# A hybrid encoder block on one core: the mixer's projections and chains in another order, and the small-weight terms of the half products last

## The chip, the cores and the metric

The kernel runs on one NeuronCore of a Trainium2 chip. The metric is the device time of one execution in microseconds (us); lower is better. The core's engines work through instruction lists of their own, each in its order, and wait for each other by semaphores: PE (TensorE, matmuls; its weight loads are counted apart as PEld), DVE (VectorE), ACT (ScalarE), POOL (GpSimd) and SP (SyncE, which issues the weights' DMAs).

## The reference

One encoder block on 512 tokens and 16 learned meta tokens (528 in all), model width 1024, all in float32:

```python
h = h + 0.5 * swiglu(rms_norm(h, ffn1_norm), w_gate1, w_up1, w_down1)      # D_FF = 2816
u = rms_norm(h, mix_norm)
z = u @ w_in                                   # split into 10 parts, below
y_a = hgrn2_bidir(zq_a, zi_a, zf_f, zf_b, zg_a, ...)   # 4 heads of 128, chunks of 128, both directions
y_b = axial_gqa(zq_b, zk_b, zv_b, q_norm, k_norm, cos, sin)   # 8 query heads of 64, 2 key heads
mixed = sigmoid(zgate_a) * (y_a @ w_up_a) + sigmoid(zgate_b) * (y_b @ w_up_b)
h = h + mixed @ w_out
h = h + 0.5 * swiglu(rms_norm(h, ffn2_norm), w_gate2, w_up2, w_down2)
return h[:, N_META:]
```

## The kernel before

Activations lie transposed, features on the 128 partitions and tokens along the free axis. Every weight and activation of a product is split into a large part (`whi`, `xh`: float32 rounded to float32r) and the small rest (`wlo`, `xl`); a product is three matmuls, hi x xh, hi x xl and lo x xh. A weight block of 128 x 1024 is loaded by SP, its `whi` is cast by ACT and its `wlo` subtracted by DVE (`Weights`); two buffers of each.

**The FFNs.** Hidden columns come in groups; all but the first four use a Strassen-like scheme with seven products of halves for gate (i = 0) and up (i = 1) each (`pair`, `step`, `product`). `product` is twelve matmuls into one PSUM bank: four blocks kk of 128 rows, three terms each. Outside the mixer a scheduler orders the instructions of each engine.

**The mixer** is ordered by a planner while the program is written (`Order`, called `il`). It keeps a clock `t` for PE and a time at which each other engine is free; `account` adds an estimated cost per instruction, `HOP` is its estimate for passing a result to another engine and `DRAIN` for a matmul's result to be there. The main stream is the projections `u @ w_in` (`group`, 24 matmuls for 512 tokens, or twice as many narrower ones for all 528, which need two of the three `mm` banks of PSUM). Chains are Python generators: `prepare` (norms and rotary positions of queries and keys, values), `scores` (matmul into bank S, softmax), `turned` (transposes of the probabilities into `at`, product with the values into an `mm` bank, `ta`, `yb`), `gla` (the recurrence: per head seven levels, each a matmul `gs<-Z,ks`, DVE updates of Z, tot and A, and ACT's copy `ks`), `gla_finish`. `tick` after each three terms of a projection lets every chain step that is ready by then be written (`pump`); `need` makes the main stream stand still until a condition holds. So the planner alone sets the order of every engine's list in the mixer; at run time the engines follow these lists.

The main stream before: the queries' projection of head 0, keys, backward gate, values, forward gate and the rest of head 0; then per head hd an output gate's projection (`early`), the wait for the scores of head hd - 2, and that head's six projections. At its end, the wait for `attention`, the split of all four `yb` into `ybh` and `ybl`, and eight products with them (`branch`), gated by `mixb`.

Of the kernel before, what the change touches and what calls it, by code (L numbers as in the profile page):

```python
# [32 lines left out]
WARM = 12  # L33
LEVELS = (1, 2, 4, 8, 16, 32, 64)
# [119 lines left out]
class Chain:  # L154


    def __init__(self, gen, ready):
        self.gen, self.ready, self.eng, self.wait = gen, ready, None, None


class Order:
# [4 lines left out]
    HOP, DRAIN = 0.12, 0.3  # L166
# [7 lines left out]
    def account(self, eng, op, args, kw):  # L174
# [15 lines left out]
        if eng == "act":  # L190
            d = n * 0.000916 + 0.115
            if "accum_out" in kw:
                d += 0.2
            if not isinstance(kw.get("scale", 1.0), (int, float)):
                d += 0.17
# [18 lines left out]
    def add(self, gen):  # L214
        self.chains.append(Chain(gen, self.cur.ready))
# [21 lines left out]
    def tick(self, _=None):  # L237
        self.pump()
# [54 lines left out]
def block_kernel(tc, xT, wg1, wu1, wd1, w_in, wup, wout, wg2, wu2, wd2, params,  # L293
# [5 lines left out]
    def group(outs, w, xs, tick=None):  # L299
        hi, lo = w  # L300
        n = len(xs)
        for k in range(n):
            sl = slice(k * P, (k + 1) * P)
            xh, xl = xs[k]
            for i, (a, b) in enumerate(((hi, xh), (hi, xl), (lo, xh))):
                for o, cols in outs:
                    pe.matmul(o, a[:, sl], b[:, cols], start=(k == 0 and i == 0),  # L307
                              stop=(k == n - 1 and i == 2))
            if tick:
                tick(0.65 if len(outs) == 1 else 0.68)  # L310

    with (tc.tile_pool(name="persist", bufs=1) as sp, tc.tile_pool(name="wts", bufs=1) as wp,
# [157 lines left out]
        def pair(ft, xq, n):  # L470
# [113 lines left out]
        with tc.tile_pool(name="f1", bufs=1) as ft:  # L584
# [40 lines left out]
            order = [Z_QB, Z_KB, Z_FB, Z_VB, Z_FF, Z_QA, Z_G, Z_I]  # L625
            for hd in range(1, HEADS):
                order += [Z_GB + hd - 2] if hd > 1 else []
                order += [c + hd for c in (Z_QB, Z_FB, Z_FF, Z_QA, Z_G, Z_I)]
            plan = [w_in[c] for c in order]
            tiles = [w_in[Z_GB + c] for c in range(KT)] + [wup[c][:, 512:] for c in range(KT)]  # L630
            plan += tiles[HEADS - 2:EARLY] + tiles[KT:KT + 5] + tiles[EARLY:KT] + tiles[KT + 5:]
# [7 lines left out]
        with tc.tile_pool(name="mix", bufs=1) as mp, tc.manual_schedule(engines={pe.engine}):  # L639
# [3 lines left out]
            def zcols(n):  # L643
# [6 lines left out]
                group(outs, w, um, il.tick)  # L650
# [11 lines left out]
            def weights():  # L662
# [4 lines left out]
                w = W.ready.pop(0)  # L667
                if not W.ready:
# [6 lines left out]
                return w  # L675
# [36 lines left out]
            with (tc.tile_pool(name="heads", bufs=1) as hp, tc.tile_pool(name="small", bufs=1) as mn,  # L712
# [3 lines left out]
                oml, noml = lower_bounds()  # L716
# [619 lines left out]
```

## Time and profile before

| | |
|---|---|
| median of 3 runs | 1191.2 us (1189.47 to 1192.89) |
| the profiled execution | 1190.44 us, span of the trace 1188.6 us |
| busy time of PE / DVE / ACT / POOL | 1166.7 / 865.0 / 578.5 / 98.6 us |
| mean granted TensorE clock | 0.997 |
| the mixer in the trace | from 376.6 to about 727 us |

Busy time is the union of an engine's records. Matmuls are pipelined and their ends are modelled, so a busy PE is not always PE at its steady pace; the time from one start to the next tells that.

### The profile page before, as it was taken

How to read it: one execution, taken by the hardware profiler on the slowest of the kernel's cores; microseconds unless marked ns; L12 is line 12 of the kernel's file. 1: busy time of each engine (PE TensorE's matmuls, PEld its weight loads, DVE VectorE, ACT ScalarE, POOL GpSimd, SP SyncE). 2: the span in 40 equal slices, each digit the busy share in tenths (PEclk: the TensorE clock that was granted, in tenths of full speed). 3: DMA queues.
4: the chain of work that ended last, by engine and by line, in shares of the span. 5: the costliest groups of instructions: out<-in, count | busy, mean ns of one | idle time of the engine just before them, and what ended most of it. 6: DMA issues, size and time to landing. Idle time of an engine off the chain costs nothing.

```text
span 1188.6 us, 19335 instructions
## 1 busy us (share of the span) xinstructions
PE 1166.7 (98%) x7765; PEld 1068.4 (90%) x7765; DVE 865.0 (73%) x1409; ACT 578.5 (49%) x981; POOL 98.6 (8%) x77
## 2 busy tenths in 40 slices
PE   8999999999999999999999989999999999999998
PEld 8999999999999889888888868888879998998997
DVE  7988848847956779797886855454888956966863
ACT  5545525524545366757657553334444634533541
POOL 1001001001103000000000000213001101101100
PEclk9999999999999999999999999999999999999999
DMA  6233322322223221112111012332423233323213
GB/s 235 63 97 133 98 90 89 113 83 107 68 67 116 75 86 57 51 37 71 37 54 53 28 45 98 107 109 95 142 64 132 85 106 110 105 91 109 90 56 123
DMA packets 34233, 106.21 MB, mean 89 GB/s; under 512 B 3936, under 2 KB 4320, under 8 KB 34144
## 3 DMA queue, kind: packets, MB, share of 16 engines
q1 hardware_dynamic: 33984, 104.44, 26.4%
q8 instruction: 61, 1.00, 0.3%
q0 software_dynamic: 160, 0.54, 0.1%
q14 instruction: 28, 0.23, 0.1%
HBM read 102.87 MB, written 2.10 MB: 88 GB/s over the span
## 4 chain that ended last, share of the span: by engine, by line
PE 90%; DVE 5%; ACT 2%; DMA 2%; issue 1%; SPq 0%; POOL 0%; ACTq 0%; DVEq 0%
PE mm L289 21%; PE mm L307 20%; PE mm L484 14%; PE at L484 9%; PE at L307 5%; PE am L307 4%; PE gs L484 4%; PE S L307 4%; PE gs L289 3%; PE am L484 2%; DVE wlo L102 1%; PE S L289 1%; PE at L289 1%; DMA raw<-in_wu 1%; ACT whi L101 1%
## 5 line engine op out<-in xcount | busy, mean ns | idle before, releaser
L101 ACT CAST whi<-raw 128x1024 fp32r<-128x1024 f32 (+2 forms) x179 | 149.9, 839 | 254.2 <-PE mm L307 87.3
L102 DVE TENSOR_TENSOR wlo<-raw,whi 128x1024 fp32r<-128x1024 f32 (+2 forms) x179 | 176.9, 991 | 22.1 <-ACT whi L101 20.0
L289 PE MATMUL mm<-xh,whi 128*128 128x512 f32 (+1 forms) x352 | 115.1, 364 | 1.6 <-DVE tm L289 1.2
L289 PE MATMUL mm<-xh,wlo 128*128 128x512 f32 (+1 forms) x352 | 108.8, 346 | 0.0
L289 PE MATMUL mm<-xl,whi 128*128 128x512 f32 (+1 forms) x352 | 108.6, 346 | 0.0
L102 DVE TENSOR_TENSOR wlo<-sums,whi 128x1024 fp32r<-128x1024 f32 x72 | 87.5, 1217 | 25.3 <-ACT whi L101 25.2
L101 ACT CAST whi<-sums 128x1024 fp32r<-128x1024 f32 x72 | 75.4, 1050 | 62.0 <-DVE sums L128 21.0
L133 POOL TENSOR_TENSOR sums<-raw 128x512 f32<-128x512 f32 x36 | 57.9, 1608 | 495.1 <-DVE wlo L102 485.8
L289 PEld LDWEIGHTS mm<-xh,whi 128*128 128x128 f32 x352 | 62.4, 191 | 9.9 <-DVE tm L289 2.0
L289 PEld LDWEIGHTS mm<-xh,wlo 128*128 128x128 f32 x352 | 62.0, 191 | 8.4
L289 PEld LDWEIGHTS mm<-xl,whi 128*128 128x128 f32 x352 | 62.1, 191 | 4.9
L307 PE MATMUL mm<-hh,wlo 128*128 128x256 f32 (+1 forms) x218 | 63.0, 334 | 0.0
L307 PE MATMUL mm<-hh,whi 128*128 128x256 f32 (+1 forms) x218 | 62.9, 333 | 0.1
L307 PE MATMUL mm<-hl,whi 128*128 128x256 f32 (+1 forms) x218 | 62.9, 332 | 0.0
L484 PE MATMUL mm<-xl,whi 128*128 128x264 f32 (+1 forms) x216 | 61.3, 284 | 0.0
L484 PE MATMUL mm<-xh,whi 128*128 128x264 f32 (+1 forms) x216 | 61.2, 284 | 0.0
L484 PE MATMUL mm<-xh,wlo 128*128 128x264 f32 (+1 forms) x216 | 61.2, 283 | 0.0
L289 ACT CAST whi<-raw 128x1024 fp32r<-128x1024 f32 (+1 forms) x41 | 39.6, 965 | 38.9 <-PE mm L289 32.5
L307 PE MATMUL mm<-xl,whi 128*128 128x512 f32 (+2 forms) x152 | 51.1, 362 | 1.3 <-DVE xl L389 1.3
L307 PE MATMUL mm<-xh,whi 128*128 128x512 f32 (+2 forms) x152 | 50.4, 357 | 1.8 <-ACT xh L388 1.8
L578 DVE SCALAR_TENSOR_TENSOR h<-mm,h 128x512 f32<-128x512 f32 (+2 forms) x40 | 20.9, 544 | 41.4 <-PE mm L307 41.3
L289 DVE TENSOR_TENSOR Z<-Z,tot 128x512 f32<-128x512 f32 (+1 forms) x48 | 40.7, 875 | 13.8 <-PE gs L289 6.8
(354 smaller groups left out, 3593.2 us busy)
## 6 DMA issues: line engine op xcount, KB each, us to landing
raw<-in_wg SPq DMA_DIRECT2D x43, 512.0 KB, 3.6
raw<-in_wu SPq DMA_DIRECT2D x43, 512.0 KB, 3.3
raw<-in_w_in SPq DMA_DIRECT2D x42, 512.0 KB, 3.2
raw<-in_wd SPq DMA_DIRECT2D x48, 384.0 KB, 3.1
raw<-in_wd SPq DMA_DIRECT2D x16, 256.0 KB, 2.6
raw<-in_wup SPq DMA_DIRECT2D x16, 256.0 KB, 2.6
raw<-in_wout SPq DMA_DIRECT2D x8, 512.0 KB, 3.3
h<-in_xT SPq DMA_DIRECT2D x4, 528.0 KB, 5.7
```

What stands on the lines that cost most here:

```text
L101: nc.scalar.copy(hi[:, c], src)
L102: nc.vector.tensor_tensor(lo[:, c], src, hi[:, c].bitcast(F32), ALU.subtract)
L133: nc.gpsimd.tensor_tensor(t[:, E], r0[:, E], r1[:, E], ALU.add)
L289: return f(*args, **kw)
L307: pe.matmul(o, a[:, sl], b[:, cols], start=(k == 0 and i == 0), stop=(k == n - 1 and i == 2))
L484: pe.matmul(o, a[:, sl], b[:, kk, :], start=(start and kk == 0 and i == 0), stop=(kk == 3 and i == 2), skip_group_check=True)
L578: dve.scalar_tensor_tensor(h[c][:, cols], o, 0.5, h[c][:, cols], ALU.mult, ALU.add)
```

## The change

Three things are altered. In `product` the four matmuls with the weight's small part come after the eight with its large part. In the planner, the costs are other ones (HOP and DRAIN, two of ACT's, DVE taken as busy until 6.5 us after the start), ready chains are looked for after every matmul instead of every third, and of chains that are ready, the two of the recurrence win by a lead of 5 us. And the mixer's program is another: the projections follow a list (`MAIN`: q, k, w are queries, keys, values, b, f, a, g, i the recurrence's, s an output gate), the wait for a head's scores moves from the main stream into the chain of the queries (`queries_rest`), the sum of a head's two halves becomes a chain of its own (`summed`), the split of a head's output follows at once (`parted`, into buffers that are free by then: `kh0` and `kl0`, `cossin`, two `qst`), and the first branch begins with three heads before the fourth is there.

```diff
-    HOP, DRAIN = 0.12, 0.3
+    HOP, DRAIN = 0.06, 0.12
...
     def pump(self):
         while self.chains:
-            ch = min(self.chains, key=self.ready)
+            ch = min(self.chains, key=lambda ch: self.ready(ch) - (ch.lead if self.ready(ch) <= self.t else 0.0))
...
             for i, (a, b) in enumerate(((hi, xh), (hi, xl), (lo, xh))):
                 for o, cols in outs:
                     pe.matmul(o, a[:, sl], b[:, cols], start=(k == 0 and i == 0),
-                              stop=(k == n - 1 and i == 2))
-            if tick:
-                tick(0.65 if len(outs) == 1 else 0.68)
+                              stop=(k == (HEADS if ks else n) - 1 and i == 2))
+                if tick:
+                    tick()
...
-                for kk in range(4):
-                    sl = slice(half * 512 + kk * P, half * 512 + (kk + 1) * P)
-                    for i, (a, b) in enumerate(((hi, xh), (hi, xl), (lo, xh))):
-                        pe.matmul(o, a[:, sl], b[:, kk, :], start=(start and kk == 0 and i == 0),
-                                  stop=(kk == 3 and i == 2), skip_group_check=True)
+                terms = [(kk, hi, x) for kk in range(4) for x in (xh, xl)] + [(kk, lo, xh) for kk in range(4)]
+                for i, (kk, a, b) in enumerate(terms):
+                    pe.matmul(o, a[:, half * 512 + kk * P:half * 512 + (kk + 1) * P], b[:, kk, :],
+                              start=(start and i == 0), stop=(i == 11), skip_group_check=True)
...
+MAIN = """q0 k0 b0 f0 a0 w0 g0 i0 b1 f1 q1 a1 g1 i1 q2 s0 q3 s1 b2 f2 a2 g2 i2 b3 f3 a3 g3 i3 s2""".split()
...
                     act.activation(tq[:, :SEQ], z[:, :SEQ], AF.Square)
+                    if j > 1:
+                        yield lambda: f"att{j - 2}" in il.done
...
-                            yield
-                            act.copy(t[d], av[s])
-                            yield
-                            dve.tensor_tensor(yb[j][d], av[d], t[d], ALU.add)
-                            give()
+                            il.add(summed(j, e, av, t, d, s))
...
+                def parted(j):
+
+                    yield lambda: {"att1", f"q{HEADS - 1}", f"att{j}"} <= il.done
...
+                    act.copy(both[0], yb[j])
+                    yield
+                    dve.tensor_tensor(both[1], yb[j], both[0].bitcast(F32), ALU.subtract)
...
-                for hd in range(1, HEADS):
-                    if hd > 1:
-                        early(hd - 2)
-                        il.need(lambda: f"att{hd - 2}" in il.done)
-                    queries(hd)
-                    for _ in gla_inputs(hd):
-                        pass
...
-                il.need(lambda: "attention" in il.done)
-                YB = []
-                ybh = hp.tile([P, 4, SEQ], F32R, name="ybh", tag="ph")
-                ybl = hp.tile([P, 4, SEQ], F32R, name="ybl", tag="pl")
...
+                il.need(lambda: f"y{HEADS - 2}" in il.done)
+                begun = [branch(range(HEADS - 1), go_on=c + 1 < BEGUN) for c in range(BEGUN)]
+                il.need(lambda: f"y{HEADS - 1}" in il.done)
```

Where this moves instructions is seen in the engines' lists. A row is the line of the kernel, the operation, out<-in and the shape, with the engines that it waits for.

First PE's list in an FFN, where a later group of hidden columns begins: before, the end of the gate's second product (`mm<-b21`) and the beginning of up's first (`at<-b11`):

```order
L484 MATMUL mm<-b21h,whi 128x264
L484 MATMUL mm<-b21l,whi 128x264
L484 MATMUL mm<-b21h,wlo 128x264
L484 MATMUL at<-b11h,whi 128x264 [waits Activation_49]
L484 MATMUL at<-b11l,whi 128x264
L484 MATMUL at<-b11h,wlo 128x264 [waits DVE_49]
```

After, the end of up's first product and the beginning of its second (`am<-b21`); three more pairs `at<-b11h,whi` and `at<-b11l,whi` stand ahead of these rows:

```order
L485 MATMUL at<-b11h,whi 128x264
L485 MATMUL at<-b11l,whi 128x264
L485 MATMUL at<-b11h,wlo 128x264 [waits DVE_49]
L485 MATMUL at<-b11h,wlo 128x264 x3
L485 MATMUL am<-b21h,whi 128x264
L485 MATMUL am<-b21l,whi 128x264
```

The wait for DVE, which makes `wlo`, stood at the third matmul of the product and stands at the ninth.

Then PE's list in the mixer behind the product of head 0's second half with its values (`pmeta` is the last matmul of that). Before:

```order
L289 MATMUL mm<-pmeta,vs_4869 128x512 [waits DVE_49]
L289 MATMUL gs<-Z,ks 128x128 [waits DVE_49,Activation_49]
L289 MATMUL gs<-Z,ks 128x128 x3
L289 MATMUL at<-ident,pr 128x128 x4
L289 MATMUL am<-ident,pr 16x128
L289 MATMUL S<-kh_4807,qst 128x256
L289 MATMUL S<-kh_4807,qst 128x272
L289 MATMUL S<-kl_4808,qst 128x256
L289 MATMUL S<-kl_4808,qst 128x272
L289 MATMUL mm<-ident,on 128x128 [waits DVE_49,Activation_49]
L289 MATMUL mm<-ident,on 128x128 [waits Activation_49] x3
L289 MATMUL mm<-kones,tq 128x2 [waits Activation_49]
```

After:

```order
L291 MATMUL mm<-pmeta,vs_4854 128x512
L291 MATMUL gs<-zi,ks 128x128 [waits DVE_49,Activation_49]
L291 MATMUL gs<-zi,ks 128x128 x3
L291 MATMUL mm<-xh,whi 128x512
L291 MATMUL mm<-xl,whi 128x512
L291 MATMUL mm<-xh,wlo 128x512
L291 MATMUL mm<-vt,A 128x128 [waits DVE_49]
L291 MATMUL mm<-vt,A 128x128
L291 MATMUL mm<-st,Z 128x128 x2
L291 MATMUL mm<-vt,A 128x128 x2
```

Before, a level of the recurrence, the next transposes, scores, `on` and the norm `kones` of the next queries follow with no projection (`mm<-xh,whi`) among them. Now projection matmuls stand behind the recurrence's first product; the outputs (`vt,A`), one score and a norm follow, 22 matmuls, and then projections again.

Last PE's list where the attention ends. Before, from the last matmul of the last head's output to the first branch:

```order
L289 MATMUL mm<-pmeta,vs_4870 128x512 [waits DVE_49]
L289 MATMUL mm<-vt,st 128x128
L289 MATMUL mm<-vt,on 128x128 [waits Activation_49]
L289 MATMUL mm<-vt,on 128x128 x3
L289 MATMUL mm<-ybh,whi 128x512 [waits PE_49,Activation_49]
L289 MATMUL mm<-ybl,whi 128x512 [waits DVE_49]
L289 MATMUL mm<-ybh,wlo 128x512
```

After, in the first branch, which begins behind the last head's output with one projection matmul, four transposes of Z and two projection matmuls between (`kh`, `kl` and `cossin` hold heads 0 and 1, `qst` heads 2 and 3):

```order
L291 MATMUL mm<-kh_6440,whi 128x512
L291 MATMUL mm<-kl_6441,whi 128x512
L291 MATMUL mm<-kh_6440,wlo 128x512
L291 MATMUL mm<-cossin,whi 128x512 x2
L291 MATMUL mm<-cossin,wlo 128x512
L291 MATMUL mm<-qst,whi 128x512 x2
L291 MATMUL mm<-qst,wlo 128x512
L291 MATMUL mm<-ident,Z 16x128 [waits DVE_49]
L291 MATMUL mm<-qst,whi 128x512 [waits Activation_49]
L291 MATMUL mm<-qst,whi 128x512 [waits DVE_49]
L291 MATMUL mm<-ident,Z 128x128 x4
L291 MATMUL mm<-qst,wlo 128x512
```

Before, each head's large and small part is waited for in turn, all four of them; after, only the last head's two parts are, behind nine matmuls with the other three. In ACT's list the four casts `ybh<-yb` stood together; now one cast `qst<-yb` stands there. The norm of the first queries (`kones`) stands behind twelve pairs of matmuls of the keys' projection before and behind ten after.

## Rows read from the trace of the kernel before

**Rows 1.** The page's busy time: engine, busy us (share of the span), instructions.
```profile
PE 1166.7 (98%) x7765; PEld 1068.4 (90%) x7765; DVE 865.0 (73%) x1409; ACT 578.5 (49%) x981; POOL 98.6 (8%) x77
```

**Rows 2.** Windows: stretch, length, PE, PEld, DVE, ACT, POOL busy (instructions), PEclk, DMA.
```profile
376.60:393.10 16.50, 15.04 (x87) 13.54 (x86) 12.27 (x30) 6.50 (x11) 2.09 (x6) 0.90 0.30 104
...
389.70:393.00 3.30, 3.30 (x17) 3.30 (x17) 1.83 (x10) 0.08 (x1) 0.00 (x0) 0.50 0.29 109
...
476.00:516.00 40.00, 37.14 (x233) 31.46 (x232) 30.23 (x62) 26.28 (x57) 0.22 (x2) 1.00 0.09 34
...
684.00:708.00 24.00, 19.92 (x102) 14.89 (x101) 13.13 (x31) 13.28 (x33) 0.00 (x0) 1.00 0.08 24
...
760.00:800.00 40.00, 40.00 (x177) 32.83 (x176) 20.67 (x25) 14.58 (x21) 7.97 (x5) 1.00 0.32 111
```

**Rows 3.** Timeline of PE in the FFNs: start, length, operation [idle before <-releaser].
```profile
184.02 0.28 PE L484 MATMUL at<-b11h,whi 128*128 128x264 f32 x1
184.14 0.28 PE L484 MATMUL at<-b11l,whi 128*128 128x264 f32 x1
185.08 0.39 PE L484 MATMUL at<-b11h,wlo 128*128 128x264 f32 x1 [0.65 <-DVE wlo L102]
...
282.87 0.39 PE L484 MATMUL at<-b11h,wlo 128*128 128x264 f32 x1 [0.68 <-DVE wlo L102]
...
907.19 0.39 PE L484 MATMUL at<-b11h,wlo 128*128 128x256 f32 x1 [0.52 <-DVE wlo L102]
...
86.21 0.39 PE L484 MATMUL at<-b11h,wlo 128*128 128x264 f32 x1 [0.33 <-DVE wlo L102]
```

**Rows 4.** Timeline of PE at the mixer's start, and ACT's tq.
```profile
387.68 1.02 PE L289 MATMUL mm<-kones,tq 128*128 128x2 f32 x8 [1.46 <-issue]
388.89 0.41 PE L289 MATMUL mm<-xl,whi 128*128 128x256 f32 x2
...
391.37 0.64 PE L289 MATMUL mm<-xh,wlo 128*128 128x256 f32 x2
...
386.95 0.63 ACT L289 ACTIVATE tq<-tm 128x512 f32<-128x512 f32 x1 [2.43 <-DVE tm L289]
```

**Rows 5.** Timeline of PE in the mixer, two waits.
```profile
405.40 0.74 PE L289 MATMUL mm<-xh,whi 128*128 128x256 f32 x2 [0.39 <-DVE tm L289]
...
508.34 1.20 PE L289 MATMUL gs<-Z,ks 128*128 128x128 f32 x8 [0.61 <-ACT ta L289]
```

**Rows 6.** Timeline of PE and of ACT around 604 us.
```profile
604.03 1.52 PE L289 MATMUL gs<-Z,ks 128*128 128x128 f32 x8 [1.41 <-ACT ks L289]
...
605.77 0.63 PE L289 MATMUL mm<-xl,whi 128*128 128x512 f32 x1
...
601.73 0.58 ACT L289 COPY ta<-mm 64x512 f32<-64x512 f32 x1 [2.33 <-PE mm L289]
602.41 1.04 ACT L289 CAST whi<-raw 128x1024 fp32r<-128x1024 f32 x1
603.36 0.61 ACT L289 COPY ks<-Z 128x512 f32<-128x512 f32 x1
```

**Rows 7.** Timeline of PE, ACT and DVE at the end of attention.
```profile
691.79 0.50 PE L289 MATMUL mm<-ybh,whi 128*128 128x512 f32 x1 [1.04 <-ACT ybh L289]
...
697.14 0.50 PE L289 MATMUL mm<-ybh,wlo 128*128 128x512 f32 x1 [1.32 <-DVE wlo L289]
...
706.87 0.51 PE L289 MATMUL mm<-ybh,wlo 128*128 128x512 f32 x1 [0.75 <-DVE wlo L289]
...
691.11 2.19 ACT L289 CAST ybh<-yb 128x512 fp32r<-128x512 f32 x4
...
691.77 2.50 DVE L289 TENSOR_TENSOR ybl<-yb,ybh 128x512 fp32r<-128x512 f32 x4 [1.18 <-ACT ybh L289]
```

**Rows 8.** Timeline of the last head's transposes on PE and their input on ACT.
```profile
710.00 0.60 PE L289 MATMUL mm<-ident,on 128*128 128x128 f32 x4
...
706.30 1.14 ACT L289 ACTIVATE on<-mm,yo 128x128 f32<-128x128 f32 x4 [0.23 <-DVE yo L289]
```

More of the change, by code (lines that the diff above doesn't have):

```diff
@@ L33 @@
 WARM = 12
+R_READY = 6.5
+LEAD = 5.0
+BEGUN = 1
+MAIN = """q0 k0 b0 f0 a0 w0 g0 i0 b1 f1 q1 a1 g1 i1 q2 s0 q3 s1 b2 f2 a2 g2 i2 b3 f3 a3 g3 i3 s2""".split()
+AMONG = sum(m[0] == "s" for m in MAIN)
 LEVELS = (1, 2, 4, 8, 16, 32, 64)
@@ L154, with __init__ @@
 class Chain:
-    def __init__(self, gen, ready):
-        self.gen, self.ready, self.eng, self.wait = gen, ready, None, None
+    def __init__(self, gen, ready, lead=0.0):
+        self.gen, self.ready, self.eng, self.wait, self.lead = gen, ready, None, None, lead
 class Order:
-    HOP, DRAIN = 0.12, 0.3
+    HOP, DRAIN = 0.06, 0.12
     def __init__(self):
@@ L212, in account, with add @@
         cur.eng = eng
-    def add(self, gen):
-        self.chains.append(Chain(gen, self.cur.ready))
+    def add(self, gen, lead=0.0):
+        self.chains.append(Chain(gen, self.cur.ready, lead))
     def ready(self, ch):
@@ L674, in weights @@
                     W.fetch()
-                return w
             def scaled(dst, outs):
@@ L1172, in early @@
                     sgs.append(sg)
-                for gen in (prepare(), scores(), turned(), gla(), gla_finish()):
-                    il.add(gen)
-                queries(0)
-                gi = gla_inputs(0)
-                kz, ksq = tmp("keys"), hp.tile([P, TP], F32, name="ksq", tag="pr", bufs=3)[:, :T]
-                scaled(kz, zcols(T))
-                main_input("keys", (kz, ksq))
-                next(gi)
-                vz = tmp("values")
-                scaled(vz, zcols(T))
-                main_input("values", vz)
@@ L1201, in block_kernel @@
-                for c in range(HEADS - 2, EARLY):
-                    early(c)
-                il.need(lambda: "attention" in il.done)
-                YB = []
-                ybh = hp.tile([P, 4, SEQ], F32R, name="ybh", tag="ph")
-                ybl = hp.tile([P, 4, SEQ], F32R, name="ybl", tag="pl")
-                ready = il.t
-                for j, y in enumerate(yb):
-                    il.main.ready = ready
-                    split((ybh[:, j, :], ybl[:, j, :]), y, slice(0, SEQ))
-                    YB.append((ybh[:, j, :], ybl[:, j, :]))
+                for gen, lead in ((prepare(), 0.0), (scores(), 0.0), (turned(), 0.0), (gla(), LEAD), (gla_finish(), LEAD)):
+                    il.add(gen, lead)
@@ new lines, in keys, with values @@
+                def keys():
+                    kz, ksq = tmp("keys"), hp.tile([P, TP], F32, name="ksq", tag="pr", bufs=3)[:, :T]
+                    scaled(kz, zcols(T))
+                    main_input("keys", (kz, ksq))
+                def values():
+                    vz = tmp("values")
+                    scaled(vz, zcols(T))
+                    main_input("values", vz)
+                gi = [gla_inputs(hd) for hd in range(HEADS)]
+                for m in MAIN:
+                    what, j = m[0], int(m[1])
+                    if what in "qs":
+                        (queries if what == "q" else early)(j)
+                    elif what in "kw":
+                        (keys if what == "k" else values)()
+                    else:
+                        next(gi[j], None)
@@ L1217, in block_kernel @@
                         gate(sgs[-1])
-                    b = branch(YB)
+                    b = branch(range(HEADS - 1, HEADS), *begun[c]) if c < BEGUN else branch(range(HEADS))
+                    if c == 0:
+                        ahead()
                     act.activation(sgs[c], sgs[c], AF.Sigmoid)
```

61 lines of the change are left out of this document (40 added, 21 removed).

## The prediction, made before the run

> **What bounds the kernel now.** The busy times come first: PE is busy for 1166.7 of 1188.6 us [rows 1], so whatever the change gives must come out of PE's idle time, or out of time in which PE runs below its rate. Next I cut the span into stretches. The stretch from 760 on, plain 512-column products, has no idle time at all [rows 2], and it holds 177 matmuls in 40 us, 0.226 us each; the FFNs are like it but for a few single waits. The mixer (376.6 to about 727 us) has the rest: 1.46 us idle in its first 16.5 us, 2.86 in the 40 us from 476 on, 4.08 in the 24 us from 684 on [rows 2]. A wait costs more than the idle time that the timeline prints. In the FFN at 184 us one product starts 0.12 us behind the one before it, the next 0.94 us later, where 0.65 us are shown as idle [rows 3]: 0.82 us are lost, the idle time and about 0.17 more. I add those 0.17 us to each wait below.
>
> The Trainium skill ("Trainium Kernel Development and Optimization", Performance Expectations) says that a matmul's busy time is a bad measure of what is left, and that the busy share of weight loads is a good one. By it the stretch from 760 on would still have 18% to give, since its loads are busy for 32.83 of 40 us; its rows have PE at its steady pace there, so I do not count that as room.
>
> **FFN products.** The instructions and their number stay; each product of 12 matmuls now has its eight with the weight's large part first and the four with the small part (wlo) last. The first matmul that needs wlo becomes the ninth instead of the third, six matmuls or 6 x 0.12 = 0.73 us later. Only waits for wlo can shrink: 0.65, 0.68 and 0.52 us of idle at 185.08, 282.87 and 907.19 [rows 3], or 0.82, 0.85 and 0.69 us lost. Each gives back the smaller of its loss and 0.73: 0.73 + 0.73 + 0.69 = 2.15. At 86.21 a further wait (0.33 idle, 0.50 lost) had three other products' matmuls woven in as cover; now eight matmuls of this product stand there, which cover about 0.24 us more. Together **-2.4 us**. What is late next is the next weight, split on ACT and DVE; no wait follows these places in the trace, so I let the gain stand. Bounds: 0 (the same DVE is late again a few products on) to 2.7 (all four gone).
>
> **The mixer's start.** The first queries' norm needs tq, which ACT makes from 386.95 to 387.58, whatever PE does; the kones matmuls start at 387.68 after 1.46 us idle [rows 4]. They stand behind twelve pairs of the key projection before the change and behind ten after it (the planner looks more often). Two pairs, 1,056 columns or 0.47 us at 0.226 us for 512, are moved from before that wait to behind it: **+0.5 us**. From 389.7 to 393.0 the granted clock was 0.50 [rows 2], the lower level of 1.2 GHz, and the records of a pair's matmuls took 0.64 instead of 0.41 us [rows 4]: 3.3 us at half pace lose 1.65 us. PE had idled for 1.46 us shortly before. With 2 us of idle I expect that again, at no difference.
>
> **Projections in another order.** Before, two 528-token projections (values, then forward gate) stand side by side; each takes two of three PSUM banks, and the second waits for an eviction, 0.39 + 0.17 us [rows 5]. After, no two are neighbours: **-0.5**.
>
> **The hold for a head's scores.** Before, the main stream may not write the projection of head 2's queries until the scores of head 0 are issued, and then chains run alone on PE. There the chains' own latencies show: PE waits for ACT 0.61 us at 508.34 [rows 5], and the stretch from 476 to 516 has 2.86 us idle [rows 2], about 3.5 lost with four times 0.17. After, this condition stands inside the queries' own chain, and projection matmuls follow the head's outputs at once. Some of it is bank waits that stay; I take two thirds, **-2.3** (bounds 0 and 3.5).
>
> **ACT's queue at 604 us.** PE waits 1.41 us for ks, which ACT copied from 603.36 on; ahead of it in ACT's order stood ta, which waited for PE's outputs, and a whole weight's whi of 1.04 us [rows 6]. Behind it the clock is low again (0.63 us for a product at 605.77). Loss: 1.41 + 0.17 + 1.65 = 3.2. Now outputs are summed in a chain of their own and the recurrence has a lead of 5 us where both are ready; in ACT's new order only one ks still follows a ta closely, against three. I take **-2.6** (bounds 0 and 3.2).
>
> **The end of attention.** Before, PE waits for the first split of the heads' outputs, for the weight behind them and once more for a weight [rows 7]; with a wait at 686.94 the stretch has 4.08 us idle [rows 2], with four times 0.17 4.8 lost. After, three heads are split long before, the fourth alone stays. Behind its last output matmul PE has 12 products of 0.226 us and four short ones in float32, eight records (four take 0.60 us with their tail [rows 8], so some 0.9): 3.6 us. ACT's ta (0.58 [rows 6]), DVE's sum (a step of 512 columns, 0.62 by the four of [rows 7]) and ACT's cast (0.55, a quarter of 2.19 [rows 7]) make the split's large part some 2.2 us behind that matmul, with hops: no wait. The small part has two updates of the state and an eviction before it on DVE: 1.5 us for ta and sum, three steps and its own, 2.5, with hops about 4.3, while PE asks at about 4.0. I leave 0.4 us for it. Two weights' wlo still stand behind an eviction or the twelve short DVE steps of the norm (0.75 us idle at 706.87 [rows 7]); 0.7 us for them. So 1.1 of 4.8 us stay: **-3.7** (bounds -2 and -4.8).
>
> **The tighter planner.** Its hops go from 0.12 to 0.06 and PE's drain from 0.3 to 0.12, and it looks for ready chains after each matmul instead of each third. A round trip from PE over DVE and ACT back to PE is thus issued about 0.3 us earlier, and 0.23 more by the mean wait for a look. Of the 141 chain pieces on PE whose input I could match (from kones at 387.68, 0.10 us behind tq's end [rows 4], to the transposes at 710.00, 2.56 us behind on's end [rows 8]), five start within 0.2 us of their input, and those are the waits above; all others have 0.51 us or more. Taking 0.6 us from each makes three more late, by 0.24 us in all. I charge **+0.6** (bounds 0.2 and 2).
>
> **Sum.** -2.4 + 0.5 - 0.5 - 2.3 - 2.6 - 3.7 + 0.6 = -10.4. The profiled run took 1190.44 us, so 1180.0; the median of the runs is 0.76 higher, 1191.2, so 1180.8. No DMA is moved on SP's queue: its list is the same before and after. A measurement of this kernel tells about 0.3% (3.6 us) from nothing.
>
> **Rivals.**
> (a) *The clock does not fall at the start, or falls elsewhere too.* Each fall costs 1.65 us. For it speaks that the waits at 691.79 and 697.14 [rows 7], of over 1 us each, left the clock at 1.00 in their stretch [rows 2]; against it, that the clock fell behind both waits of 1.4 us and more. One fall less gives 1179, two more 1184. The Trainium skill ("TensorE: Matmul & The Clock Gate", Part 1) says that the monitor runs free of the kernel, so where a wait falls decides too; the trace bears that out so far as waits of like length differ.
> (b) *Only fixed places gain.* The waits at 508 and 604 belong to one interleaving; the new one has its own, in other places. Then FFN, banks and tail remain: -2.4 + 0.5 - 0.5 - 3.7 + 0.6 = -5.5, 1185.7.
> (c) *No change.* As (b), and the tail keeps half its waits, because the last split still follows DVE's state updates, and the FFN's DVE is late again: -1.2 + 0.5 - 1.8 + 0.6 = -1.9, 1189.
> (d) *Slower: the planner without margin.* If the pieces' slack was the old constants' and not the engines', all 141 come late by some amount x, 141x in all; at x = 0.10 us, 14 us, the change is 3.6 us slower, 1195. Against it stand the 0.51 us found at all but five pieces.
>
> **Numbers.** The forecast, -7.5 to -14, has 0.57, more than that 0.07, (b) 0.2, (c) 0.09, (d) 0.07; (a) lies inside the forecast's own range, 1177 to 1184. All recoverable waits gone, and one fall of the clock with them, would be -2.7 - 0.5 - 3.5 - 3.2 - 4.8 - 1.65 + 0.7 = -15.7, 1175.5; a little below it lies the lower end, 1174. The upper end, 1188, takes in (b) and some new waits. Faster by over 0.3%: 0.57 + 0.07 + most of (b) = 0.83; same 0.10; slower 0.07.
>
> **What would show it.** The four waits for wlo at FFN groups' starts shrink below 0.2 us (one 0.3). The first kones matmul waits about 2 us, a slow stretch behind it. No stretch of the mixer longer than 6 us without a projection's matmul; no wait of over 1 us for ks; about 1 us of waits from the last head's outputs to the gates' end. Wrong would make it: many PE waits of 0.1 to 0.3 us on ACT spread over the mixer, more than two stretches at 1.2 GHz, or waits for whi in the branches, where the weight behind the begun branch is fetched only at its end.

## The result, and the profile after

The changed kernel takes 1182.07 us (median of 4 runs, 1180.24 to 1182.4) against 1190.74 us before on the same chip: a ratio of 0.9922, 95% interval 0.9904 to 0.994. The forecast was 1181 us, within 1174 to 1188, so the time came as predicted; several terms of the sum did not. The profiled execution took 1182.03 us, its trace 1180.2 us. The page's busy time, against [rows 1]:

```profile
PE 1164.1 (99%) x7765; PEld 1070.4 (91%) x7765; DVE 868.7 (74%) x1409; ACT 578.5 (49%) x981; POOL 95.3 (8%) x77
```

Windows of the kernel after, columns as in [rows 2]:

```profile
160.00:320.00 160.00, 160.00 (x1310) 159.77 (x1309) 118.19 (x166) 70.84 (x107) 15.38 (x11) 1.00 0.29 97
376.90:393.40 16.50, 14.55 (x82) 13.05 (x81) 13.04 (x31) 6.33 (x10) 2.14 (x7) 0.90 0.33 110
476.00:516.00 40.00, 40.00 (x253) 35.16 (x252) 32.40 (x72) 23.42 (x46) 0.22 (x2) 1.00 0.15 53
560.00:576.00 16.00, 14.21 (x90) 12.64 (x89) 13.12 (x32) 12.17 (x29) 0.41 (x1) 0.89 0.09 34
600.00:612.00 12.00, 11.93 (x70) 10.01 (x69) 11.90 (x17) 6.58 (x14) 0.00 (x0) 1.00 0.17 52
684.00:708.00 24.00, 21.27 (x113) 16.99 (x112) 11.60 (x27) 11.18 (x28) 0.00 (x0) 1.00 0.19 67
```

Windows of the kernel before that [rows 2] does not have:

```profile
160.00:320.00 160.00, 158.66 (x1296) 157.93 (x1295) 116.84 (x164) 69.99 (x106) 15.37 (x11) 1.00 0.29 95
560.00:576.00 16.00, 15.62 (x102) 13.10 (x101) 11.77 (x29) 11.14 (x32) 0.11 (x1) 1.00 0.10 34
600.00:612.00 12.00, 10.59 (x50) 8.57 (x49) 9.17 (x16) 5.53 (x10) 0.00 (x0) 0.86 0.22 82
```

Read them pairwise. From 160 to 320 us PE has no idle time left and 14 matmuls more. From 476 to 516 the 2.86 us of idle time [rows 2] are gone; from 600 to 612 the wait for ks [rows 6] and the low clock behind it are gone too. But from 560 to 576 PE now idles for 1.79 us where it idled for 0.38, with the clock low for a part of it, and the end of attention keeps 2.73 of 4.08 us. PE's three longest waits in the mixer, and the short one right behind the second, timeline of PE after:

```profile
388.01 1.02 PE L291 MATMUL mm<-kones,tq 128*128 128x2 f32 x8 [1.95 <-issue]
568.97 0.38 PE L291 MATMUL mm<-xh,whi 128*128 128x256 f32 x1 [1.45 <-DVE zi L291]
569.70 0.40 PE L291 MATMUL mm<-xh,whi 128*128 128x272 f32 x1 [0.34 <-DVE yb L291]
690.57 0.50 PE L291 MATMUL mm<-kh,wlo 128*128 128x512 f32 x1 [2.16 <-DVE wlo L291]
```

The first was forecast (2 us, [rows 4]). The second is new: a 528-token projection needs two banks, and DVE evicts them late. DVE after, at that place:

```profile
564.51 0.17 DVE L291 TENSOR_SCALAR xo<-ss 128x4 f32<-128x4 f32 x1 [1.89 <-ACT on L291]
...
566.77 0.70 DVE L291 TENSOR_REDUCE nm<-S 128x1 f32<-128x528 f32 x1
567.51 0.69 DVE L291 TENSOR_TENSOR qst<-tm,qst 64x512 fp32r<-64x512 f32 x1
568.22 0.69 DVE L291 TENSOR_TENSOR zi<-mm,R 128x512 f32<-128x512 f32 x1
```

DVE idles for 1.89 us, waiting for ACT, before the twelve short steps of the recurrence's norm, goes through them and two more, and only then evicts zi, for which PE has waited since its last product, which began at 567.04. The last wait is in the second branch. ACT and DVE after:

```profile
686.62 0.62 ACT L291 CAST whi<-raw 128x512 fp32r<-128x512 f32 x1
687.26 1.28 ACT L291 ACT_TABLE_LOAD   x1
688.56 0.63 ACT L291 ACTIVATE mixb<-mixb 128x512 f32<-128x512 f32 x1
...
689.22 0.69 DVE L291 TENSOR_TENSOR mixb<-mm,mixb 128x512 f32<-128x512 f32 x1 [4.11 <-ACT mixb L291]
689.83 1.28 DVE L291 TENSOR_TENSOR wlo<-raw,whi 128x512 fp32r<-128x512 f32 x2
```

The weight's small part stands behind the first branch's eviction, which waits for the gate's sigmoid, and that for ACT's table load of 1.28 us.

### The profile page after: what moved, and what is told of

The parts are those of the page before. It is cut to its first block, busy times and chain, and to the rows that moved or that the text cites. A ratio compares the mean times of both kernels' runs of the same rounds, so it can differ in the third digit from the quotient of the medians.

```text
span 1180.2 us, 19335 instructions
## 1 busy us (share of the span) xinstructions
PE 1164.1 (99%) x7765; PEld 1070.4 (91%) x7765; DVE 868.7 (74%) x1409; ACT 578.5 (49%) x981; POOL 95.3 (8%) x77
## 4 chain that ended last, share of the span: by engine, by line
PE 94%; DVE 2%; DMA 2%; ACT 1%; issue 1%; SPq 0%; POOL 0%; ACTq 0%; DVEq 0%
PE mm L309 22%; PE mm L291 21%; PE mm L485 15%; PE at L485 9%; PE at L309 5%; PE am L309 5%; PE gs L485 4%; PE S L309 4%; PE gs L291 3%; PE am L485 2%; PE S L291 1%; PE at L291 1%; DMA raw<-in_wd 1%; DMA h<-in_xT 1%; ACT whi L106 0%
## 5 line engine op out<-in xcount | busy, mean ns | idle before, releaser
L291 PE MATMUL mm<-xh,whi 128*128 128x512 f32 (+1 forms) x352 | 111.9, 355 | 1.8 <-DVE zi L291 1.4
L291 PE MATMUL mm<-xl,whi 128*128 128x512 f32 (+1 forms) x352 | 111.3, 354 | 0.0
L138 POOL TENSOR_TENSOR sums<-raw 128x512 f32<-128x512 f32 x36 | 54.3, 1508 | 495.1 <-DVE wlo L107 486.5
L485 PE MATMUL mm<-xh,whi 128*128 128x264 f32 (+1 forms) x216 | 54.7, 284 | 0.0
L485 PE MATMUL mm<-xl,whi 128*128 128x264 f32 (+1 forms) x216 | 54.6, 284 | 0.0
L309 PE MATMUL mm<-xh,wlo 128*128 128x512 f32 (+2 forms) x152 | 50.9, 361 | 0.0
```

Source lines behind the costliest of these rows:

```text
L138: nc.gpsimd.tensor_tensor(t[:, E], r0[:, E], r1[:, E], ALU.add)
L291: return f(*args, **kw)
L485: pe.matmul(o, a[:, half * 512 + kk * P:half * 512 + (kk + 1) * P], b[:, kk, :], start=(start and i == 0), stop=(i == 11), skip_group_chec ...
```

## The experiments

Medians of all kernels timed. The kernel before was timed again beside them, at 1190.74 to 1191.75 us, and the ratio is to that; so differences of two kernels' medians below can be off by up to 1 us. "PE idle" is 364 us less PE's busy time in the window 376:740 of each kernel's profile, one execution, which takes in the mixer. "Stands still" is what the planner's own clock says while the program is written: how long the main stream, the projections, waits at a `need` for a chain (only those over 1 us, and without those for a weight's split, at most 2.1 us; att = a head's scores, gla = the end of a head's recurrence, y3 and attention = the last head's output). It is a plan, not a measurement.

| kernel | us (median) | ratio to before, 95% | PE idle, us (profile) | main stream stands still, us (planner) |
|---|---|---|---|---|
| before | 1191 | 1 | 11.0 | att0 6.9, gla0 6.3, attention 8.1 |
| b_product | 1187.78 | 0.9969 (0.9959 to 0.9978) | 10.7 | the same |
| b_planner | 1193.19 | 1.0018 (1.0007 to 1.0028) | 12.7 | gla0 14.2 |
| b_three | 1188.69 | 0.998 (0.9971 to 0.9989) | 12.7 | gla0 14.2 |
| **after** | 1182.07 | 0.9922 (0.9904 to 0.994) | 6.5 | none |
| a_order_old | 1181.11 | 0.9906 (0.9889 to 0.9923) | 6.6 | gla0 4.2, gla1 1.3, y3 5.0 |
| a_tail_old | 1182.84 | 0.9932 (0.9919 to 0.9945) | 7.7 | none |
| a_look3 | 1189.27 | 0.9987 (0.9977 to 0.9996) | 12.3 | y3 9.1 |
| a_planner_old | 1194.19 | 1.0017 (1.0007 to 1.0027) | 15.5 | gla0 7.8, gla1 7.7, y3 11.9 |
| a_hold | 1196.46 | 1.0044 (1.0028 to 1.0059) | 16.7 | att1 33.7 |
| a_ready8 | 1177.33 | 0.9874 (0.9861 to 0.9888) | 5.5 | none |
| a_sig | 1178.8 | 0.9888 (0.9875 to 0.9902) | 5.7 | none |
| a_r8_sig | 1176.65 | 0.9878 (0.9865 to 0.9891) | 4.6 | none |
| a_r8_sig_l0 | 1188.33 | 0.9975 (0.9965 to 0.9985) | 10.7 | gla1 19.1 |

**The products alone (b_product).** The edit is the change's `product` in the kernel before.

> The kernel before with one thing altered: in the FFNs' products the four terms with the weight's small part stand last. Theory (the prediction's term): the waits for wlo at about 184, 283 and 907 us vanish and the one at 86 us shrinks, nothing follows them: 2.4 us less than the kernel before (0.998), up to 3.5 us if what the changed kernel's FFNs show is all from this (excess over the steady pace from 160 to 320 us from 2.7 to 0.1, from 80 to 120 us 0.5 less, from 895 to 1000 us 0.4 less). Rival: the same DVE is late again a few products on, or the scheduler had it right: 0 to 1 us less, with new waits of PE for wlo of over 0.4 us between 160 and 360 us. The mixer's trace stays as before, its waits at 508, 604 and 691 us within 0.1 us.

3.4 us less, with this window:

```profile
160.00:320.00 160.00, 160.00 (x1310) 159.77 (x1309) 118.99 (x168) 71.43 (x108) 15.37 (x11) 1.00 0.30 95
```

The theory holds, at its upper figure. The two waits in this stretch print 0.65 and 0.68 us of idle time [rows 3] and lost 0.82 and 0.85 us by the prediction's reckoning; 14 matmuls of 0.12 us are 1.7 us, so about their whole loss came back, and not only the 0.73 us that the prediction took from each.

**The planner's costs alone (b_planner)**, in the kernel before:

```diff
-    HOP, DRAIN = 0.12, 0.3
+    HOP, DRAIN = 0.06, 0.12
...
-            if tick:
-                tick(0.65 if len(outs) == 1 else 0.68)
+                if tick:
+                    tick()
```

> The kernel before with the planner's new costs alone (HOP 0.06, DRAIN 0.12, the two ACT costs) and a look for ready chains after each matmul; the projections' order, the holds and the end of attention stay as before. Theory (the prediction): the costs are no source of gain and cost little, 0.6 us: within 2.5 us of the kernel before, with some wait of over 1 us still at the holds for a head's scores and 4 us or more lost between 684 and 708 us. Rival 1: the planner's costs are where the mixer's gain comes from: 4 us or more less. Rival 2 (the planner without margin): many PE waits of 0.1 to 0.3 us and 3.6 us or more longer.

2.0 us slower: no gain by itself, as the prediction had it. Nor is it rival 2: there is no spread of small waits, and the largest loss is one place, a wait of 3.95 us, the same that b_three shows below. The chains run earlier, the projections reach the inputs of the third head's recurrence sooner, and there the main stream stands for the first head's recurrence to end.

**The hold back in the main stream (a_hold)**, from the changed kernel:

```diff
-                    if j > 1:
-                        yield lambda: f"att{j - 2}" in il.done
...
+                    if what == "q" and j > 1:
+                        il.need(lambda: f"att{j - 2}" in il.done)
```

> The changed kernel with the hold for the scores of heads 0 and 1 back in the main stream, ahead of the queries' projections of heads 2 and 3, and taken out of the queries' chain. All else as changed. Theory (the prediction's term): chains run alone on PE again for some 10 us, and 2.3 us are lost there, 1184.4; with a fall of the clock behind one of the waits 1.65 us more, 1186.0. Rival: in the new interleaving the scores are ready by then, so that the hold's place means nothing: within 1 us of the changed kernel, with no stretch of over 6 us without a projection's matmul.

14.4 us slower, six times the term. First the window of all instructions and then that of the projections' operand xh alone (no POOL column), for this kernel:

```profile
508.00:538.00 30.00, 20.55 (x119) 16.50 (x119) 28.85 (x53) 20.85 (x42) 0.00 (x0) 0.89 0.00 1
...
508.00:538.00 30.00, 0.00 (x0) 0.00 (x0) 0.00 (x0) 0.00 (x0) 0.89 0.00 1
```

The same stretch of the changed kernel, xh alone:

```profile
508.00:538.00 30.00, 20.28 (x77) 12.66 (x75) 0.00 (x0) 0.00 (x0) 1.00 0.20 71
```

For 30 us no projection runs: PE idles for 9.45 us, the clock falls (0.89), and DVE is the bound, busy for 28.85 of 30 us with the chains alone. Both theories had sizes that were far too small. The price is that of the hold in the new list, though: there the queries of head 3 follow those of head 2 with one gate between, where the old order has five more projections of head 2 ahead of them, so that the hold for the scores of head 1 comes earlier and stands for 33.7 us by the planner. The hold in the main stream with the old order of the projections, all else as changed, was not run.

**The old end of attention (a_tail_old)**, from the changed kernel:

```diff
-                il.need(lambda: f"y{HEADS - 2}" in il.done)
-                begun = [branch(range(HEADS - 1), go_on=c + 1 < BEGUN) for c in range(BEGUN)]
-                il.need(lambda: f"y{HEADS - 1}" in il.done)
+                il.need(lambda: "summed" in il.done)
...
+                for j, y in enumerate(yb):
+                    il.main.ready = ready
+                    split((ybh[:, j, :], ybl[:, j, :]), y, slice(0, SEQ))
```

> The changed kernel with the end of attention as before: all four heads' outputs are split together after the last one is summed, and the first branch begins whole behind that. All else as changed. Theory (the prediction's term, 3.7 us for early splits): 3.7 us slower than the changed kernel, 1185.8, by 2.4 us if what the two traces show between 680 and 710 us (7.1 against 4.7 us over the steady pace) is all from the splits; a wait of about 1 us for ybh, and one of over 1 us for wlo. Rival: the gain at the end comes from the other order of the projections, so that fewer chains are left there: 0 to 1 us slower.

0.8 us slower, within what the runs spread: the rival. The timeline of PE says why:

```profile
677.51 0.50 PE L291 MATMUL mm<-pmeta,vs 48*128 48x512 f32 x1
...
685.46 0.40 PE L291 MATMUL mm<-ybh,whi 128*128 128x512 f32 x1
...
687.01 0.50 PE L291 MATMUL mm<-ybl,whi 128*128 128x512 f32 x1 [0.26 <-DVE ybl L291]
...
690.83 0.50 PE L291 MATMUL mm<-ybh,wlo 128*128 128x512 f32 x1 [0.53 <-DVE wlo L291]
```

Between the last head's output and the first branch stand 8 us of work, most of it the output gates' projections, which cover the splits; before, there were only three us, 1.04 of them a wait [rows 7] and most of the rest products of the recurrence. So the end gained because attention ends earlier among the projections, not by the early splits. That the splits were moved costs or gives elsewhere: this trace has a wait of 2.17 us before 657.58 us, which the changed kernel has not. At the end itself, from 676 to 712 us, it waits less than the changed kernel does, 1.8 against 2.7 us.

**The old order of the projections (a_order_old)**, from the changed kernel:

```diff
-MAIN = """q0 k0 b0 f0 a0 w0 g0 i0 b1 f1 q1 a1 g1 i1 q2 s0 q3 s1 b2 f2 a2 g2 i2 b3 f3 a3 g3 i3 s2""".split()
+MAIN = """q0 k0 b0 w0 f0 a0 g0 i0 q1 b1 f1 a1 g1 i1 s0 q2 b2 f2 a2 g2 i2 s1 q3 b3 f3 a3 g3 i3""".split()
```

> The changed kernel with its projections in the order of the kernel before (values ahead of the forward gate, each head's six projections together); the hold for a head's scores stays in the queries' chain, and all else as changed. Theory, after the run with the hold back in the main stream was 14 us slower: it is the hold's place that pays, not the order of the projections, whose own part is the wait for a bank at 405 us (0.5 in the prediction): 1182 to 1184 us, no stretch of over 6 us without a projection's matmul before the end of attention, a wait of about 0.5 us between 395 and 410 us. Rival: the order of the list is what lets the chains run beside projections: 1186 or more, with new waits of over 1 us between 480 and 640.

1181.11 us: the order by itself gives nothing measurable, as the theory had it. The wait for a bank in its place stays under 0.5 us. But the two orders lose their time in different places. This one has no idle time from 560 to 576 us, where the changed kernel has 1.79, and idles at the end instead, with the clock low; its window there:

```profile
676.00:700.00 24.00, 20.52 (x84) 15.85 (x83) 14.32 (x25) 10.42 (x17) 0.00 (x0) 0.79 0.16 55
```

Its first queries' norm waits as long as the changed kernel's, but the clock stays up, timeline of PE and a window:

```profile
386.65 1.02 PE L291 MATMUL mm<-kones,tq 128*128 128x2 f32 x8 [1.97 <-issue]
...
387.50:391.50 4.00, 4.00 (x33) 3.92 (x33) 3.38 (x16) 0.51 (x1) 0.00 (x0) 1.00 0.43 135
```

**The old costs and look (a_planner_old), and the old look alone (a_look3)**, from the changed kernel; the second has the second piece only:

```diff
-    HOP, DRAIN = 0.06, 0.12
+    HOP, DRAIN = 0.12, 0.3
...
-                if tick:
-                    tick()
+            if tick:
+                tick()
```

> The changed kernel with the planner's old costs (HOP 0.12, DRAIN 0.3, the two ACT costs) and a look after each third matmul; the lead, the start of DVE, the list and the chains stay as changed. Theory (the prediction, and the kernel before with the new costs alone, which was 0.2% slower than it): the costs give nothing of their own, so 1180 to 1184, with the wait for the first queries' norm shorter than 2.1 us since it stands behind more pairs. Rival: list and costs belong together, and chains that are started later leave PE with waits at the heads' ends: 1186 or more.

> The changed kernel with one thing altered: the planner looks for ready chains after each third matmul of a projection, as before the change, and not after each; HOP, DRAIN and the two ACT costs stay new. With the old costs and this look together it was 12 us slower. Theory 1: the look is the smaller part; the first half head's product with its values stands 5 us of PE's time later in the list than in the changed kernel, against 12 with the old costs too, so some 5 us of the 12 come back: 1187. Theory 2: only where a chain runs out of projections does it cost, and the list has no stretch without a projection over 7 us: within 2 us of the changed kernel, 1182 to 1184. Theory 3: the look is all of it: 1192 or more.

12.1 and 7.2 us slower. For the first, the rival is right; for the second theory 1 in that 4.9 of the 12.1 us come back, though the look is then more than the smaller part. The timeline of PE with old costs and look:

```profile
519.10 0.52 PE L291 MATMUL S<-kh,qst 128*128 128x256 f32 x2 [1.03 <-ACT pr L291]
...
523.56 0.73 PE L291 MATMUL mm<-ident,on 128*128 128x128 f32 x2 [1.94 <-ACT on L291]
...
697.04 0.51 PE L291 MATMUL mm<-kh,whi 128*128 128x512 f32 x1 [1.10 <-ACT whi L291]
...
702.57 0.80 PE L291 MATMUL mm<-kh,wlo 128*128 128x512 f32 x1 [4.79 <-DVE wlo L291]
```

And with the old look alone:

```profile
699.74 0.79 PE L291 MATMUL mm<-kh,wlo 128*128 128x512 f32 x1 [4.79 <-DVE wlo L291]
```

The chains' steps are written later among the projections, so the projections are used up before the chains, and what is left of the chains runs alone: with the old costs no matmul with xh runs from 515 to 524 us, at the stop for gla0, nor from 690 to 704. At the end, in both traces, the table load, the norm's twelve steps and the weight follow each other with nothing beside them.

**Three things of the change in the kernel before (b_three):** `product`, the costs and look, and the hold in the queries' chain.

> The kernel before with three things of the change: the products' order, the planner's new costs with a look after each matmul, and the hold for a head's scores in the queries' chain. The projections' order, the sum of two halves inside its chain, no lead, DVE's start and the end of attention stay as before. Theory (after the runs so far): hold and costs together are the mixer's gain, each alone gives nothing; so with the products' 3.4 us this comes to within 2 us of the changed kernel, 1181 to 1184. Rival: the sum's own chain and the recurrence's lead are needed too, since the list still has one stretch of some 9 us of PE's time without a projection, around the third head's scores; two to four us are lost there, and the end keeps most of its 4.8: 1185 to 1188.

1188.69 us: the theory falls. PE's list in the mixer is row for row that of b_planner: with the new costs the scores are there in time, and the hold does not bind wherever it stands. What binds is the recurrence of the first head, and PE waits there:

```profile
514.85 1.09 PE L289 MATMUL at<-ident,pr 128*128 128x128 f32 x4 [3.95 <-DVE pl L289]
```

Against b_planner it gains 4.5 us. The mixers' lists being the same, that is the products' order, worth 3.4 us alone.

**The first norm later (a_ready8).** `R_READY = 8.0` for 6.5.

> The changed kernel with one number altered: DVE is taken as busy until 8.0 us after the mixer's start and not 6.5, so that the first queries' norm stands behind 16 pairs of the keys' projection and not 10, 2.7 us later. Theory: the wait of 2.1 us there goes, and with it the fall of the clock behind it (3.4 us at 1.2 GHz, 1.7 us lost): 3.8 us less than the changed kernel if what stands behind is not worse. Rival 1: the fall comes from the waits at the FFN's end that come before, so that 2.1 us are won and the clock falls at the same place: 2.1 us less. Rival 2: all later chains of the first head come later, and what is won here is lost at the next waits: within 1 us.

4.7 us less, the theory's figure or a little more. The timeline of PE at the start and at the new wait, and a window behind the latter:

```profile
386.99 1.02 PE L291 MATMUL mm<-kones,tq 128*128 128x2 f32 x8 [0.50 <-issue]
...
565.67 0.39 PE L291 MATMUL mm<-xh,whi 128*128 128x256 f32 x1 [1.46 <-DVE zi L291]
...
566.00:570.00 4.00, 3.66 (x30) 3.60 (x30) 3.94 (x9) 3.91 (x9) 0.00 (x0) 1.00 0.21 48
```

1.45 us of idle time are won at the start, and in this execution the clock fell at neither place. The other executions agree: the mean granted clock over the span was 0.998 or 0.999 in all four runs of this kernel and 0.993 to 0.995 in the four of the changed kernel.

**The first sigmoid earlier (a_sig):**

```diff
                 il.need(lambda: f"y{HEADS - 1}" in il.done)
+                act.activation(sgs[0], sgs[0], AF.Sigmoid)
...
-                    act.activation(sgs[c], sgs[c], AF.Sigmoid)
+                    if c:
+                        act.activation(sgs[c], sgs[c], AF.Sigmoid)
```

> The changed kernel with the sigmoid of the first branch's gate written ahead of that branch's last head and not behind the branch, so that ACT's table load (1.28 us) and the sigmoid (0.63) stand behind the last cast of a head's output and not between the branch's last matmul and its eviction. Theory: the wait of 2.16 us for wlo in the second branch is DVE standing behind that eviction, so it falls to about 0.6 us (wlo then waits for whi and for the eviction's own 0.7): 1.5 to 2 us less than the changed kernel. Rival: wlo is late because of ACT's order in any case (the table load now delays the copies of the recurrence's state and the weight's whi): a wait of 1.5 us or more remains in the second branch, no gain.

3.3 us less. The wait is a quarter of what it was; timeline of PE and DVE:

```profile
685.47 0.50 PE L291 MATMUL mm<-kh,wlo 128*128 128x512 f32 x1 [0.56 <-DVE wlo L291]
...
697.17 0.50 PE L291 MATMUL mm<-kh,wlo 128*128 128x512 f32 x1 [1.24 <-DVE wlo L291]
...
684.13 0.69 DVE L291 TENSOR_TENSOR mixb<-mm,mixb 128x512 f32<-128x512 f32 x1 [0.89 <-ACT whi L291]
```

So the table load and the sigmoid in front of the eviction are the cause of that wait. Of the 1.6 us won there 0.9 remain, since a wait for wlo in a later branch, behind the norm's twelve steps, grew from 0.50 us to the 1.24 shown. In the profile the clock also did not fall behind the first norm; how much of the 3.3 us that is was not tried.

**Both, and both without the lead (a_r8_sig, a_r8_sig_l0).** The first has the two edits above, the second `LEAD = 0.0` too.

> The changed kernel with both alterations that helped alone: DVE's start at 8.0, and the first branch's sigmoid ahead of that branch's last head. Theory: they lie 300 us apart and add up, 2.1 us and the fall of the clock behind it at the start, some 1 to 1.5 us at the end: 1176 us, faster than the changed kernel by 0.5%. Rival: the clock's falls come at chance behind any wait of 1.5 us or more, so that one won at the start comes back at the wait of 1.7 us near 565 us: 1178 to 1179.

> As the kernel with DVE's start at 8.0 and the early sigmoid, and the recurrence without its lead of 5 us, so that of ready chains the one that is ready first is written first, as before the change. Theory (the prediction's reason for the term at 604 us): without the lead a copy ks stands behind a sum of two halves that waits for PE, so waits for ks of over 1 us come back, and the recurrence is left over at the end: 3 us or more slower than the same kernel with the lead. Rival: the lead does little or costs, since the wait near 565 us is DVE standing in twelve short steps of the recurrence's norm that the lead put ahead of an eviction: that wait goes, 1 to 3 us less.

1176.65 us for the first, the fastest by its median, 5.4 us below the changed kernel; but a_ready8 alone is within the spread (and the fastest by the ratio), so that the two gains do not add up measurably. In its profile the clock falls behind the same wait at 565 us that left it up in a_ready8:

```profile
565.66 0.39 PE L291 MATMUL mm<-xh,whi 128*128 128x256 f32 x1 [1.45 <-DVE zi L291]
...
566.00:570.00 4.00, 3.66 (x18) 3.61 (x18) 3.87 (x9) 3.91 (x9) 0.00 (x0) 0.59 0.17 43
```

Without the lead the kernel is 11.7 us slower. Its windows, all instructions and xh alone:

```profile
563.50:583.00 19.50, 14.24 (x85) 12.31 (x84) 14.28 (x37) 15.20 (x40) 0.22 (x2) 0.82 0.00 0
...
563.50:583.00 19.50, 0.03 (x1) 0.00 (x0) 0.00 (x0) 0.00 (x0) 0.82 0.00 0
```

Again a stretch without a projection, here until the second head's recurrence has ended: 5.3 us idle, and the clock down. The theory was right that it is slower and wrong in the reason: no wait for ks of over 1 us came back; the main stream waits for the recurrence. The rival was right that the wait for zi goes, and wrong that this decides.

## Why the prediction was right, and where its steps were not

*FFN products, -2.4.* Right in mechanism; 3.4 us measured (2.6 to 4.9 by the interval). I took at most 0.73 us from each printed wait, and nearly the whole losses came back. The starts of the matmuls have further losses of 0.1 us at most later groups, which print no idle time; they went too.

*The mixer's start, +0.5.* Right: the wait printed 1.46 us [rows 4] and prints 1.95, and the low clock behind it is there again (0.90 in the window, as before).

*Another order of the projections, -0.5.* The wait at 405 us is gone, but the old order costs nothing in the end: no gain of its own.

*The hold, -2.3.* The stretch gave 2.86 us of idle time, so the size fits what the rows of before show. As the value of that edit it was wrong: put back into the new list, it costs 14.4 us, and moved in the kernel before, with the new costs, it gives nothing.

*ACT's queue at 604 us, -2.6.* There the wait is gone and the clock up, but 1.4 us more idle time and a fall of the clock stand at 568 us: given back by another order of DVE. The lead, meant for this wait, pays through the recurrence's end instead (11.7 us).

*The end of attention, -3.7.* Mis-sized. Idle time went from 4.08 to 2.73 us. The step that failed is "0.7 us for two weights' wlo": I counted an eviction ahead of them, not the table load and the sigmoid that the eviction waits for; the wait was 2.16 us. And the early splits, to which I put the gain, are worth 0.8 us by a_tail_old, no more than the spread.

*The tighter planner, +0.6.* The failed step. I counted what pieces lose that come too early, and not what all chains gain by starting earlier: in the changed program the old costs and look cost 12.1 us. In the old program the new ones cost 2.0 us, since another stop takes over. No spread of small waits came, so rival (d) fell as its 0.51 us of slack said.

Rival (b) had half of it: the new interleaving did bring its own wait, at 568 us, and the stretch from 476 to 516 us gained all the same. Of the signs, the first norm's wait and the FFNs' waits came as forecast and no wait for ks of over 1 us was left. The longest stretch without a projection ahead of the branches was 6.2 us (from 559.8), where 6 was the limit and 12.5 stood before. But the waits at the end were 2.7 us and not about 1, and the profile has three stretches at 1.2 GHz, one of them at the FFN's start, where "more than two" was to speak against it. As an estimate by the prediction's own measure (idle time, 0.17 us for each wait, 1.65 for each fall of the clock) the terms came to -3.4, +0.5, -0.5, -3.5, 0, -1.7 and 0, together -8.6 us, and 8.7 were measured. So I read rightly where the time is, off the stretches of the trace; that the sum also came close is in part luck, since two terms (604 us and the end) gave some 4.6 us less than forecast and three others (the products, the hold, the planner) 2.8 more.

The edits behind the terms do not add up. In the mixer each of three things, the hold in the chain (with the new list), the lead (undone in the fastest kernel), and the costs with the look, gives back 12 to 14 us when it alone is undone, and the look alone 7.2: each more than all that the mixer gained (1187.78 to 1182.07, 5.7 us). The common mechanism, shown by the windows without projections: PE is full as long as projections are left to write beside the chains. A stop of the main stream, or chains that lag behind it, leaves them alone, and then the chains' own steps on DVE and ACT set the pace. Where the stop goes when one is lifted (att0, then gla0, then the end) goes with the time, and the changed program has none left. The planned stops do not give the time by a fixed rate: a_order_old has 10.5 us of them and loses nothing, a_look3 has 9.1 and loses 7.2. The traces tell them apart, windows of a_order_old and then of a_look3:

```profile
376.00:740.00 364.00, 357.40 (x2145) 310.17 (x2145) 281.56 (x542) 208.62 (x397) 6.16 (x15) 0.99 0.19 62
376.00:740.00 364.00, 351.66 (x2117) 306.77 (x2116) 277.99 (x537) 206.59 (x393) 4.57 (x15) 0.98 0.18 60
```

PE idles for 6.6 us in the one, as in the changed kernel, and for 12.3 in the other. So a planned stop is a place to look at, and the idle time in the trace is what it cost; why so little of a_order_old's stops became idle time is open. Nor was it tried which of the lead and the split of the sum (`summed`) lifts gla0 in the old order.

## What to carry to other kernels

Where a main stream covers dependent chains, look for the places at which it has to stop for them. Let the program print these, and hold them against PE's idle time in a trace: one stop left over can undo the rest, and edits that lift stops must be judged together. A chain's slack at each step says that starting it earlier is safe, but its value lies in where the chain ends relative to its cover. And ahead of an eviction look at what its other operand waits for: a table load of 1.28 us on ACT became 2.16 us on PE.

## What was not expected of the hardware

Behind like waits the clock fell in some executions and not in others. After the first norm's wait of 1.95 to 1.97 us it fell in the changed kernel (0.90 in the window from 376.90) and stayed at 1.00 in a_order_old; after the wait for zi, 1.45 and 1.46 us in two kernels with the same rows there, the mean of the next four us was 0.59 in one and 1.00 in the other. So rival (a) cannot be settled by the length of a wait, and the place of a fall in one profile is no property of a kernel. The mean clock over the span, on record for every run, is nearer to one: 0.993 to 0.995 in four runs of the changed kernel, 0.998 and 0.999 in four of a_ready8, 0.997 and 0.998 in four of a_r8_sig, and less firmly 0.994 to 0.997 in eleven of b_product.

The first products, whose code is the same in all these kernels, start at different times, and the clock differs there too. Before and after, timeline of PE and windows:

```profile
7.15 0.51 PE L307 MATMUL mm<-xh,whi 128*128 128x256 f32 x2 [1.80 <-ACT xh L388]
...
7.00:16.00 9.00, 8.26 (x61) 7.62 (x62) 7.80 (x11) 9.00 (x17) 1.98 (x2) 1.00 0.96 368
```

```profile
9.01 0.81 PE L309 MATMUL mm<-xh,whi 128*128 128x256 f32 x2 [3.59 <-ACT xh L390]
...
7.00:16.00 9.00, 6.99 (x36) 6.69 (x37) 5.96 (x8) 7.78 (x14) 1.32 (x1) 0.62 0.82 313
```

The profile after thus lost some 2 us more at its start than that of before, which hides the FFN's gain when the two mixers' starts (376.6 and 376.9 us) are compared.
